# Two transformer blocks on one core: the first rows of each stage by tokens, between the halves of its norm, and three held rows

## The chip, the cores and the metric

The kernel runs on one core of one Trainium2 chip. The metric is device microseconds of one execution, lower being better. The programs are written for the engines TensorE (PE, matrix products), VectorE (DVE), ScalarE (ACT), GpSimd (POOL) and SyncE (SP, which issues most transfers). A scheduler sets the order of each engine's list when the program is built; each engine then works through its list.

## The reference

256 tokens of 1,024 numbers pass through two blocks, each a mixer and a retrieval from 16,384 single-neuron experts ("Peer"). All is float32. Cut to what matters:

```python
# block 1
h = rmsnorm(x, norm_mix_g);  proj = h @ w_in            # 28 tiles of 128 columns
# retention heads (rq, rk, rv, rg) and differential attention heads (dq, dk, dv)
x = x + concatenate([ret_out, diff_out]) @ w_out
x = x + peer(rmsnorm(x, norm_ffn_g), peer_wq, peer_subkeys, peer_u, peer_v)
x = rmsnorm(x, final_norm_g)
# block 2
h = rmsnorm(x, norm1);       proj = h @ w_in_2          # gated delta rule (a_*), hgrn (b_*), gates
mix = sigmoid(g_a) * (o_a @ w_branch_a) + sigmoid(g_b) * (o_b @ w_branch_b)
x = x + mix @ w_out_2
x = x + peer(rmsnorm(x, norm2), w_pq, sub_keys, expert_u, expert_v)
return rmsnorm(x, final_norm)

def peer(x, wq, keys, u, v):
    q = x @ wq                                   # 8 heads x 2 halves x 128
    # top 16 of each half's scores, top 16 of their 256 sums, softmax: gates
    h = gelu(x @ u.T)                            # of the chosen experts
    return (gate * h) @ v
```

## The kernel before

**Stages and rows.** Five stages follow one another: mix1, Peer 1, mix2, Peer 2 and the output. Each streams its weights as rows: a row is one block of 128 x 1024 float32, 512 KB. `plan` lists 684 of them. A row passes through three steps (`_dma`, `_conv`, lines 147 to 168):

- SP fetches it into one of three buffers `raw` (line 151);
- ACT copies it to `hi`, a rounded fp32r value (line 159);
- DVE, and POOL for the last 384 columns in most stages, subtract to get `lo = raw - hi` (line 164).

`hi` and `lo` have three buffers each (the ring). `prefetch(ahead)` converts rows until `ahead` of them lie ahead of use, and issues fetches up to three rows beyond the last conversion. A fetch waits until its buffer's `lo` is done, a conversion until PE has finished with the ring's place.

**Products.** All large products are three fp32r products, hi·hi, hi·lo and lo·hi. `tile_ch` (line 197) makes one tile of 128 output columns for 256 tokens from one row: the weights are stationary, the tokens move, 24 matmuls of 256 columns. `acc_tile` (line 278) is for the output products: the tokens are stationary, the weights move, and a row is added to four PSUM banks `y` by 12 matmuls of 512 columns. At the end of each such stage the last `LAST` = 2 rows are held: `acc_held(0)` adds both to the first 128 tokens, `acc_held(1)` then to the second, so that the first tokens' norm can start while PE works on the second.

**Seams.** A norm (`norm`, `norm_twice`, `norm_first`, `final`) adds `y` to `x` on DVE (lines 289, 291), squares on ACT (296), multiplies by the gain on DVE, makes the reciprocal root on POOL (308) and a diagonal on DVE (300). PE multiplies by it, which transposes and scales at once (323), ACT and DVE evict the result as `xh` and `xl` (325, 326). Both halves of the tokens are normed, then the stage's first row is multiplied. One row of the next stage is converted ahead of the norm, the others behind its last eviction (`prefetch_behind`).

**Background work.** Heads of the mixers, top-k searches and gates are generators. `pass_round` and `step` advance them between rows; they share six PSUM banks. In mix1, `ch`/`cl` are the hi and lo parts of the heads' outputs, the stationary operand of its output projection. In mix2, `mh`/`ml` are those of the gated sum, whose column j comes from branch row b_j, so that branch rows and rows of the output projection alternate.

**Peer.** 16 query rows, 128 rows `u` and 128 rows `v`; in the last part `ah`/`al` are the hi and lo parts of an expert row's activations (lines 634, 635).

## Time and profile before

| what | value |
|---|---|
| median of 3 runs | 2221.36 us (2220.66 to 2223.72) |
| the profiled execution's own time | 2218.6 us |
| its span | 2216.8 us |
| mean granted TensorE clock, as a share of full speed | 0.996 |
| busy: PE, DVE, ACT, POOL | 2167.8, 1533.0, 1154.8, 813.5 us |

A row of a timeline gives the start, the time it took, the engine, the line of the kernel, the operation, the tile written and the tiles read, and in brackets how long the engine had been idle before it and what ended the wait. A row with xN stands for N instructions that follow one another; its time is that of all. The time of one matmul is from its start to its modelled end; matmuls overlap, and how fast they go is read from the distance of their starts.

### The profile page before, as it was taken

The page shows a single profiled execution, that of the slowest core. Times are in us where ns is not written, and L with a number is a line of the kernel's source. Part 1 is how long each engine was busy: PE and PEld are TensorE (multiplying, and loading weights), DVE is VectorE, ACT ScalarE, POOL GpSimd, SP SyncE. Part 2 cuts the span into 40 slices and gives each one's busy share as a digit, 9 for nine tenths or more (in the row PEclk, how much of TensorE's full clock was granted, in tenths as well). Part 3 has the DMA queues.
Part 4 walks back from the last instruction along what each step waited for, and adds up shares of the span by engine and source line. Part 5 has one row for each costly group of instructions (what it writes and reads, how often), then busy time and mean ns, then how long its engine had stood idle before and what let it go on. Part 6 is the DMA issues. An engine that isn't in the chain of part 4 may idle for free. (4 is left out here: it accounts for less than half of the span.)

```text
span 2216.8 us, 41395 instructions
## 1 busy us (share of the span) xinstructions
PE 2167.8 (98%) x15512; PEld 2016.0 (91%) x15512; DVE 1533.0 (69%) x3122; ACT 1154.8 (52%) x2183; POOL 813.5 (37%) x623
## 2 busy tenths in 40 slices
PE   8999999999999999989999999999999999999998
PEld 8989999999988888879899998999999999888887
DVE  5669986898644544477687787799778885444444
ACT  5645545444455555556455655455454445555554
POOL 3454000000065666646275675620000002665664
PEclk9999999999999999999999999999999999999999
DMA  5555655555556656534444244555555555665654
GB/s 188 155 176 162 185 170 167 157 162 161 172 190 207 200 192 196 193 118 137 131 123 135 68 143 152 173 162 185 178 162 158 157 160 183 193 206 190 195 194 152
DMA packets 103880, 370.89 MB, mean 167 GB/s; under 512 B 12928, under 2 KB 14080, under 8 KB 103424
## 3 DMA queue, kind: packets, MB, share of 16 engines
q1 hardware_dynamic: 101808, 365.21, 52.1%
q10 hardware_dynamic: 1872, 3.04, 0.5%
q8 instruction: 122, 2.00, 0.4%
q14 instruction: 78, 0.64, 0.1%
HBM read 367.16 MB, written 1.05 MB: 166 GB/s over the span
## 5 line engine op out<-in xcount | busy, mean ns | idle before, releaser
L164 POOL TENSOR_TENSOR lo<-raw,hi 128x384 fp32r<-128x384 f32 (+1 forms) x428 | 689.5, 1612 | 1309.1 <-ACT hi L159 1271.4
L159 ACT ACTIVATE hi<-raw 128x1024 fp32r<-128x1024 f32 x684 | 724.0, 1060 | 680.2 <-PE mm L197 403.4
L164 DVE TENSOR_TENSOR lo<-raw,hi 128x640 fp32r<-128x640 f32 (+1 forms) x654 | 668.0, 1022 | 313.5 <-ACT hi L159 306.2
L197 PE MATMUL mm<-xh,hi 128*128 128x256 f32 x2848 | 820.9, 288 | 4.4 <-DVE sg L866 2.9
L197 PE MATMUL mm<-xh,lo 128*128 128x256 f32 x2848 | 807.5, 284 | 0.3 <-DVE lo L164 0.2
L197 PE MATMUL mm<-xl,hi 128*128 128x256 f32 x2848 | 803.9, 282 | 0.9 <-DVE xl L326 0.7
L197 PEld LDWEIGHTS mm<-xh,hi 128*128 128x128 f32 x2848 | 538.2, 189 | 5.9 <-DVE sg L866 3.3
L197 PEld LDWEIGHTS mm<-xl,hi 128*128 128x128 f32 x2848 | 538.9, 189 | 1.8 <-DVE xl L326 1.1
L197 PEld LDWEIGHTS mm<-xh,lo 128*128 128x128 f32 x2848 | 534.8, 188 | 0.7 <-DVE lo L164 0.7
L278 PE MATMUL y<-lo,ah 128*128 128x512 f32 x1024 | 398.2, 389 | 0.0
L278 PE MATMUL y<-hi,ah 128*128 128x512 f32 x1024 | 397.4, 389 | 0.0
L278 PE MATMUL y<-hi,al 128*128 128x512 f32 x1024 | 275.9, 389 | 0.0
L635 DVE TENSOR_TENSOR al<-a,ah 128x256 fp32r<-128x256 f32 x256 | 118.1, 462 | 193.2 <-PE y L278 192.9
L278 PEld LDWEIGHTS y<-hi,al 128*128 128x128 f32 x1024 | 192.2, 188 | 39.9
L278 PEld LDWEIGHTS y<-lo,ah 128*128 128x128 f32 x1024 | 192.3, 188 | 39.8
L278 PEld LDWEIGHTS y<-hi,ah 128*128 128x128 f32 x1024 | 192.2, 188 | 39.8
L634 ACT ACTIVATE ah<-a 128x256 fp32r<-128x256 f32 x256 | 106.5, 417 | 168.3 <-PE y L278 166.7
L197 PE MATMUL wm<-xh,hi 128*128 128x256 f32 x320 | 92.1, 289 | 5.4 <-ACT sq L1059 2.1
L197 PE MATMUL wm<-xh,lo 128*128 128x256 f32 x320 | 90.6, 285 | 0.6 <-DVE lo L164 0.6
L197 PE MATMUL wm<-xl,hi 128*128 128x256 f32 x320 | 90.5, 283 | 0.3 <-DVE xl L326 0.3
L535 DVE TENSOR_TENSOR ow<-ow,w 128x1024 f16<-128x1024 f16 x128 | 87.1, 683 | 0.1
L563 ACT ACTIVATE a<-mm 128x256 f32<-128x256 f32 (+33 forms) x228 | 69.0, 302 | 0.0
(513 smaller groups left out, 2271.6 us busy)
## 6 DMA issues: line engine op xcount, KB each, us to landing
raw<-in_u_dram SPq DMA_DIRECT2D x256, 512.0 KB, 3.5
raw<-in_v_dram SPq DMA_DIRECT2D x256, 512.0 KB, 4.2
raw<-in_w_in_dram SPq DMA_DIRECT2D x108, 512.0 KB, 3.5
raw<-in_wq_dram SPq DMA_DIRECT2D x32, 512.0 KB, 3.7
raw<-in_w_out_dram SPq DMA_DIRECT2D x16, 512.0 KB, 3.6
raw<-in_w_branch_a_dram SPq DMA_DIRECT2D x8, 512.0 KB, 3.5
raw<-in_w_branch_b_dram SPq DMA_DIRECT2D x8, 512.0 KB, 3.6
skT<-in_sk_dram ACTq DMA_DIRECT2D x2, 1024.0 KB, 5.1
```

Source lines behind the costliest of these rows:

```text
L159: self.nc.scalar.activation(out=h, in_=r, func=ACTF.Copy)
L164: eng.tensor_tensor(out=l[:, a:b], in0=r[:, a:b], in1=h[:, a:b].bitcast(F32), op=ALU.subtract)
L197: self.nc.tensor.matmul(out=ps, lhsT=a[:, c, :], rhs=b, start=(c == 0 and k == 0), stop=(c == NC - 1 and k == 2))
L278: i = self.nc.tensor.matmul(out=self.y[tt][dh], lhsT=p[:, ts], rhs=q[:, ds], start=(first and m == 0), stop=(last and m == 2))
L535: nc.vector.tensor_tensor(out=ow[q], in0=ow[0], in1=some(self.w[:, q]), op=ALU.mult)
L563: nc.scalar.activation(out=a[:, s, n:T], in_=ps[:, n:T], func=ACTF.Gelu)
L634: nc.scalar.activation(out=h, in_=a, func=ACTF.Copy)
L635: nc.vector.tensor_tensor(out=l, in0=a, in1=h.bitcast(F32), op=ALU.subtract)
```

## The change

The first 512 columns (four rows) of mix1, Peer 1, mix2 and Peer 2 are computed by `tile_tok`: tokens stationary, weights moving, 12 matmuls of 512 columns per row, 6 for each half of the tokens. `seam` puts them between the norms: `prefetch(3)`, norm of the first tokens, three rows for the first tokens, norm of the second tokens, the same rows for the second tokens, then row 4 for both. Since the result has tokens on partitions, mix1's differential values and four of mix2's `b_i` heads need no transposes any more; the first four query tiles of Peer are transposed instead (8 each).

`LAST` is 3. `hold` gives the held rows a home outside the ring, and the run-ahead grows towards a stage's end, so that three rows of the next stage are converted as well. In a norm the gain is multiplied half by half, and the second tokens' work is ordered behind the first's diagonal and last eviction (`turn`). Evictions are in halves, in mix1's first norm in quarters. The rest: `gs` is spread at row 66 of V instead of 40 and multiplied at 88 instead of 60, the `lambda` values of mix1 are made by a generator, and in mix2 `delta` takes its banks in pairs and has fewer steps; the four `b_i` rows that stood after the output gate's are now the stage's first. Line numbers of the change: fetch 152, `hi` 163, `lo` 167, `tile_ch` 206, `tile_tok` 216, adds 328 and 330, squares 339, diagonal 343, evictions 372 and 373.

```diff
     def _conv(self):
         n = self.n_cv
         r = self.raw.pop(n)
-        h = self.ring.tile([P, D], FR, tag="hi", name="hi", bufs=HI)
+        if n in self.place:
+            h, l = self.place.pop(n)
+        else:
+            h, l = (self.ring.tile([P, D], FR, tag=t, name=t, bufs=b) for t, b in (("hi", HI), ("lo", LO)))
         self.nc.scalar.activation(out=h, in_=r, func=ACTF.Copy)
-        l = self.ring.tile([P, D], FR, tag="lo", name="lo", bufs=LO)
...
+    def hold(self, n, homes):
+
+        for m, pair in enumerate(homes):
+            assert self.n_use + n + m >= self.n_cv
+            self.place[self.n_use + n + m] = pair
...
+    def tile_tok(self, tt, w, n, y):
+        h, l = w
+        ts = slice(tt * P, (tt + 1) * P)
+        todo = [(x, b, c2) for x, bs in ((self.xh, (h, l)), (self.xl, (h,))) for c2 in range(2) for b in bs]
+        for m, (x, b, c2) in enumerate(todo):
+            self.last_mm = self.nc.tensor.matmul(out=y, lhsT=x[:, 2 * n + c2, ts], rhs=b[:, c2 * 512:c2 * 512 + 512],
+                                                 start=(n == 0 and m == 0), stop=(n == 3 and m == len(todo) - 1)).ins
+
+    def seam(self, norms, before=3):
+
+        self.prefetch(3)
+        norms[0]()
+        ws = [self.weights() for _ in range(3)]
+        self.quads = [self.bank([P, 512])]
+        for n in range(3):
+            if n == before:
+                norms[1]()
+            self.tile_tok(0, ws[n], n, self.quads[0][1])
+        if before == 3:
+            norms[1]()
+        self.quads.append(self.bank([P, 512]))
+        for n in range(3):
+            self.tile_tok(1, ws[n], n, self.quads[1][1])
+            with self.tc.issue_after(self.last_act):
+                self.prefetch(n + 1)
+        w = self.weights()
+        for tt in range(2):
+            self.tile_tok(tt, w, 3, self.quads[tt][1])
...
         for dh in range(2):
             hs = self.half(dh)
-            self.add_half(tt, dh, None)
-            self.square(x[:, hs], xn[:, hs], s[dh])
-        for dh in range(2):
-            hs = self.half(dh)
-            nc.vector.tensor_tensor(out=xg[:, hs], in0=x[:, hs], in1=gn[:, hs], op=ALU.mult)
+            with self.turn(tt, dh):
+                self.add_half(tt, dh, None)
+                self.square(x[:, hs], xn[:, hs], s[dh])
+                nc.vector.tensor_tensor(out=xg[:, hs], in0=x[:, hs], in1=gn[:, hs], op=ALU.mult)
...
-LAST = 2
+LAST = 3
...
                 for tt in range(2):
                     k.acc_tile(tt, w, a, n == 0, False)
                 k.step(BUD[1])
-                k.prefetch()
+                k.prefetch(2 + max(0, (n - (P - LAST - 9)) // 2))
 
             held = [(k.weights(), a) for a in last]
             i = k.acc_held(0, held)
-            k.prefetch(1)
+            k.prefetch(3)
...
-def out_proj(k, order, ch, cl, ready, last=2):
+def out_proj(k, order, ch, cl, ready, homes):
...
+    k.hold(len(order) - last, homes)
...
-            k.prefetch()
+            k.prefetch(min(3 + n, last + 3))
...
     i = k.acc_held(0, ws)
-    k.prefetch(1)
+    k.prefetch(3)
...
+        for tt, (tag, ps) in enumerate(k.quads):
+            nc.scalar.activation(out=self.bi[:, tt, 0:4, :].rearrange("p h n -> p (h n)"), in_=ps, func=ACTF.Copy)
+            k.done(tag)
...
-        for h in range(H):
+        for h in range(4, H):
             ps = k.tile_ch()
             k.spawn(self.token_value(h, ps))
             after(2)
...
-        for what, j in mix2_out_order():
+        cut = lambda t: [t[:, 4 * n:4 * n + 4, :].rearrange("p a b -> p (a b)") for n in range(2)]
+        k.hold(16 - LAST, [cut(self.oah), cut(self.oal), [self.t([P, D], f"wd{n}", FR, tag=f"dec{n}") for n in range(2)]])
+        for n, (what, j) in enumerate(mix2_out_order()):
+            ahead = 2 + min(LAST + 1, max(0, (n - 4) // 2))
```

What this does to the lists of the engines, at three places.

ACT at the end of mix1 (`hi` and `w_...` are conversions of rows, the latter of held rows in homes outside the ring; `ch` is a head's output, `xn` the norm's squares). Before:

```order
L772 ACTIVATE ch<-fy 128x256
L705 ACTIVATE rv<-by_1445 128x256
L159 ACTIVATE hi<-raw 128x1024
L756 ACTIVATE fj,fss<-bg_1484 128x128 x2
L159 ACTIVATE hi<-raw 128x1024 x4
L772 ACTIVATE ch<-fy 128x256
L159 ACTIVATE hi<-raw 128x1024
L296 ACTIVATE xn,nrm<-x 128x512 x4
```

and in the change:

```order
L844 ACTIVATE ch<-fy 128x256
L772 ACTIVATE rv<-by_1386 128x256
L163 ACTIVATE w_1407<-raw 128x1024
L163 ACTIVATE hi<-raw 128x1024 x2
L828 ACTIVATE fj,fss<-bg_1457 128x128
L163 ACTIVATE w_1409<-raw 128x1024
L828 ACTIVATE fj,fss<-bg_1457 128x128
L163 ACTIVATE w_1411<-raw 128x1024
L163 ACTIVATE hi<-raw 128x1024 x3
L844 ACTIVATE ch<-fy 128x256
L339 ACTIVATE xn,nrm<-x 128x512 x3
```

The last `ch` stood ahead of the one conversion of a Peer row; it now stands behind three of them.

ACT at the end of mix2 (`oah`, `oal` and `wd_...` are the held rows' homes, `mh` a column of the gated sum). Before:

```order
L1522 ACTIVATE mh<-by 128x256
L159 ACTIVATE hi<-raw 128x1024 x2
L1522 ACTIVATE mh<-by 128x256
L159 ACTIVATE hi<-raw 128x1024
L296 ACTIVATE xn,nrm<-x 128x512 x4
```

and in the change:

```order
L1608 ACTIVATE mh<-by 128x256
L163 ACTIVATE oah<-raw 128x1024
L163 ACTIVATE hi<-raw 128x1024
L163 ACTIVATE oal<-raw 128x1024
L1608 ACTIVATE mh<-by 128x256
L163 ACTIVATE wd_15853<-raw 128x1024
L163 ACTIVATE hi<-raw 128x1024 x3
L1608 ACTIVATE mh<-by 128x256
L339 ACTIVATE xn,nrm<-x 128x512 x3
```

The last `mh` likewise stands behind the conversions of three rows of the next stage, and these behind the last held row's.

DVE at the end of Peer 1 (`al` belongs to the last rows of V, `x<-y,x` is the norm's add). Before:

```order
L635 TENSOR_TENSOR al<-a_1722,ah 128x256
L164 TENSOR_TENSOR lo<-raw,hi 128x640 x3
L291 SCALAR_TENSOR_TENSOR x<-y,x 128x512 x2
L385 TENSOR_TENSOR a_4058<-x,a_4058 128x512
```

and in the change:

```order
L167 TENSOR_TENSOR wl_9417<-raw,wh_9416 128x640
L167 TENSOR_TENSOR lo<-raw,hi 128x640
L694 TENSOR_TENSOR al<-a_1742,ah 128x256
L167 TENSOR_TENSOR wl_9419<-raw,wh_9418 128x640
L167 TENSOR_TENSOR wl_9421<-raw,wh_9420 128x640
L167 TENSOR_TENSOR lo<-raw,hi 128x640 x3
L330 SCALAR_TENSOR_TENSOR x<-y,x 128x512 x2
L431 TENSOR_TENSOR x_9410<-x,g_9406 128x512
```

The add stood behind the conversions of two held rows and one row of mix2; it now stands behind three of each.

## Rows read from the trace of the kernel before

**Rows 1.** The page: engines' busy time; groups of instructions with mean ns and idle time.
```profile
PE 2167.8 (98%) x15512; PEld 2016.0 (91%) x15512; DVE 1533.0 (69%) x3122; ACT 1154.8 (52%) x2183; POOL 813.5 (37%) x623
...
L164 POOL TENSOR_TENSOR lo<-raw,hi 128x384 fp32r<-128x384 f32 (+1 forms) x428 | 689.5, 1612 | 1309.1 <-ACT hi L159 1271.4
L159 ACT ACTIVATE hi<-raw 128x1024 fp32r<-128x1024 f32 x684 | 724.0, 1060 | 680.2 <-PE mm L197 403.4
...
L278 PE MATMUL y<-lo,ah 128*128 128x512 f32 x1024 | 398.2, 389 | 0.0
```

**Rows 2.** Stretches: length, busy PE, PEld, DVE, ACT, POOL, then clock, DMA share, GB/s.
```profile
140.00:143.00 3.00, 0.77 (x4) 0.29 (x2) 3.00 (x8) 1.93 (x6) 0.56 (x1) 1.00 0.52 183
...
952.00:958.00 6.00, 0.41 (x3) 0.14 (x1) 5.45 (x15) 3.54 (x10) 1.08 (x3) 0.72 0.12 48
958.00:960.00 2.00, 2.00 (x10) 2.00 (x11) 0.29 (x1) 0.02 (x1) 2.00 (x3) 0.50 0.00 0
960.00:962.00 2.00, 2.00 (x13) 2.00 (x13) 0.69 (x1) 0.89 (x2) 1.23 (x2) 0.62 0.00 0
962.00:964.00 2.00, 1.66 (x15) 1.46 (x14) 1.49 (x4) 1.41 (x4) 0.36 (x1) 1.00 0.00 0
1398.00:1400.00 2.00, 0.84 (x4) 0.36 (x2) 2.00 (x5) 1.01 (x3) 0.56 (x1) 1.00 0.51 201
```

**Rows 3.** Timeline of PE, mix1 to Peer 1.
```profile
140.15 0.40 PE L278 MATMUL y<-lo,ch 128*128 128x512 f32 x1
140.38 0.39 PE L278 MATMUL y<-hi,cl 128*128 128x512 f32 x1
143.22 2.02 PE L323 MATMUL bg<-xn,xg 128*128 128x128 f32 x16 [2.45 <-DVE xn L300]
...
147.55 0.39 PE L197 MATMUL mm<-xl,hi 128*128 128x256 f32 x1 [0.34 <-DVE xl L326]
147.78 0.28 PE L197 MATMUL mm<-xh,lo 128*128 128x256 f32 x1
147.90 0.28 PE L197 MATMUL mm<-xh,hi 128*128 128x256 f32 x1
```

**Rows 4.** Timeline of PE, Peer 1 to mix2.
```profile
951.91 0.39 PE L278 MATMUL y<-hi,al 128*128 128x512 f32 x1
957.89 3.76 PE L323 MATMUL bg<-a 128*128 128x128 f32 x16 [5.59 <-issue]
...
963.95 0.39 PE L197 MATMUL wm<-xl,hi 128*128 128x256 f32 x1 [0.34 <-DVE xl L326]
```

**Rows 5.** Timeline of PE, mix2 to Peer 2.
```profile
1398.45 0.39 PE L278 MATMUL y<-hi,ml 128*128 128x512 f32 x1
1400.61 2.02 PE L323 MATMUL bg<-xn,xg 128*128 128x128 f32 x16 [1.77 <-DVE xn L300]
...
1404.94 0.39 PE L197 MATMUL mm<-xl,hi 128*128 128x256 f32 x1 [0.34 <-DVE xl L326]
```

**Rows 6.** Timeline of ACT, the output projection of mix1.
```profile
124.58 1.06 ACT L159 ACTIVATE hi<-raw 128x1024 fp32r<-128x1024 f32 x1 [3.40 <-PE y L278]
...
126.19 2.00 ACT L159 ACTIVATE hi<-raw 128x1024 fp32r<-128x1024 f32 x2
131.14 1.06 ACT L159 ACTIVATE hi<-raw 128x1024 fp32r<-128x1024 f32 x1 [2.96 <-DMA raw<-in_w_out_dram]
133.91 1.06 ACT L159 ACTIVATE hi<-raw 128x1024 fp32r<-128x1024 f32 x1 [1.71 <-DMA raw<-in_w_out_dram]
134.88 0.40 ACT L772 ACTIVATE ch<-fy 128x256 fp32r<-128x256 f32 x1
```

**Rows 7.** DMA issues from 126 to 146 us: KB each, median us from issue to landing.
```profile
raw<-in_wq_dram SPq DMA_DIRECT2D x4, 512.0 KB, 4.3
raw<-in_w_out_dram SPq DMA_DIRECT2D x2, 512.0 KB, 3.9
```

**Rows 8.** Timeline of ACT, the output projection of mix2.
```profile
1376.59 1.06 ACT L159 ACTIVATE hi<-raw 128x1024 fp32r<-128x1024 f32 x1 [1.37 <-PE y L278]
...
1390.45 1.06 ACT L159 ACTIVATE hi<-raw 128x1024 fp32r<-128x1024 f32 x1 [1.63 <-PE mm L197]
1391.44 0.42 ACT L1522 ACTIVATE mh<-by 128x256 fp32r<-128x256 f32 x1
1393.35 1.06 ACT L159 ACTIVATE hi<-raw 128x1024 fp32r<-128x1024 f32 x1 [1.49 <-PE y L278]
```

**Rows 9.** Timeline of ACT, last rows of Peer 1.
```profile
936.07 1.06 ACT L159 ACTIVATE hi<-raw 128x1024 fp32r<-128x1024 f32 x1 [0.54 <-PE y L278]
...
938.79 1.06 ACT L159 ACTIVATE hi<-raw 128x1024 fp32r<-128x1024 f32 x1 [0.54 <-PE y L278]
```

**Rows 10.** Timeline of DVE, the start of Peer 1's norm.
```profile
948.04 0.83 DVE L164 TENSOR_TENSOR lo<-raw,hi 128x640 fp32r<-128x640 f32 x1 [1.90 <-ACT hi L159]
949.17 1.29 DVE L291 SCALAR_TENSOR_TENSOR x<-y,x 128x512 f32<-128x512 f32 x2 [0.30 <-PE y L278]
```

**Rows 11.** Timeline of ACT, the output's norm.
```profile
2210.41 0.72 ACT L304 ACTIVATE a<-a,nrm 128x512 f32<-128x512 f32 x1
2211.03 0.61 ACT L296 ACTIVATE a<-x 128x512 f32<-128x512 f32 x1
```

**Rows 12.** The stretch of mix2 with its last `mx` tiles, columns as in rows 2.
```profile
1340.00:1360.00 20.00, 16.83 (x120) 14.35 (x120) 15.54 (x32) 9.79 (x30) 11.49 (x12) 1.00 0.41 147
```

More of the change, by code (lines that the diff above doesn't have):

```diff
@@ L319, in transposed @@
             tag, ps = self.bank([P, 4, P])
-            cs = slice(c4 * 4, c4 * 4 + 4)
+            with self.tc.issue_after(self.last_mm) if tt else nullcontext():
+                for c in range(4):
+                    cc = c4 * 4 + c
+                    nc.tensor.matmul(out=ps[:, c, :], lhsT=x[:, cc * P:(cc + 1) * P], rhs=dr, start=True, stop=True)
+            for c in range(0, 4, 2):
+                cs = slice(c4 * 4 + c, c4 * 4 + c + 2)
+                h, v = self.xh[:, cs, ts], ps[:, c:c + 2]
+                last = nc.scalar.activation(out=h, in_=v, func=ACTF.Copy)
+                i = nc.vector.tensor_tensor(out=self.xl[:, cs, ts], in0=v, in1=h.bitcast(F32), op=ALU.subtract).ins
@@ new lines, in transposed, with norm_first @@
+            self.done(tag)
+        self.last_act = last.ins
+        self.behind[1] = i
+    def norm_first(self, tt, g, xn):
+        nc = self.nc
+        x, s = self.x[:, tt, :], self.columns()
+        self.square(x[:, 512:D], xn[:, 512:D], s[0])
+        nc.vector.scalar_tensor_tensor(out=xn[:, 0:512], in0=x[:, 0:512], scalar=1.0 / D, in1=x[:, 0:512],
+                                       op0=ALU.mult, op1=ALU.mult, accum_out=s[1])
+        nc.vector.tensor_scalar(out=s[4], in0=s[0], scalar1=s[1], scalar2=EPS, op0=ALU.add, op1=ALU.add)
+        self.rsqrt(s[6], s[4])
+        dr = xn[:, 0:P]
+        self.diagonal(dr, s[6])
+        ts = slice(tt * P, (tt + 1) * P)
+        for c4 in range(2):
+            tag, ps = self.bank([P, 4, P])
+            with self.tc.issue_after(self.last_mm) if tt else nullcontext():
+                for c in range(4):
+                    cc = c4 * 4 + c
+                    nc.tensor.matmul(out=ps[:, c, :], lhsT=x[:, cc * P:(cc + 1) * P], rhs=dr, start=True, stop=True)
@@ L412, in final @@
             hs = self.half(dh)
-            self.add_half(tt, dh, scale)
-            self.square(x[:, hs], xn[:, hs], s[dh])
-        for dh in range(2):
-            hs = self.half(dh)
-            nc.vector.tensor_tensor(out=xg[:, hs], in0=x[:, hs], in1=gb[:, hs], op=ALU.mult)
+            with self.turn(tt, dh):
+                self.add_half(tt, dh, scale)
+                self.square(x[:, hs], xn[:, hs], s[dh])
+                nc.vector.tensor_tensor(out=xg[:, hs], in0=x[:, hs], in1=gb[:, hs], op=ALU.mult)
         nc.vector.tensor_scalar(out=s[4], in0=s[0], scalar1=s[1], scalar2=EPS, op0=ALU.add, op1=ALU.add)
@@ L736, in mix1 @@
     with k.tc.tile_pool(name="m1", bufs=1) as pool:
-        k.norm_first(k.g, [pool.tile([P, D], F32, name="xn", tag="xn", bufs=2) for tt in range(2)])
-        k.prefetch_behind()
+        k.seam([lambda tt=tt: k.norm_first(tt, k.g, pool.tile([P, D], F32, name="xn", tag="xn", bufs=2)) for tt in range(2)], 2)
+        vt = pool.tile([P, 2, 4, P], F32, name="vt")
+        for tt, (tag, ps) in enumerate(k.quads):
+            nc.scalar.activation(out=vt[:, tt].rearrange("p h n -> p (h n)"), in_=ps, func=ACTF.Copy)
+            k.done(tag)
+        k.prefetch()
         half = k.const(pool, "half", True)
@@ L1537, in run @@
         xg, xn = self.t([P, 2, D], "xg", tag="bi"), self.t([P, 2, D], "xn", tag="sgb")
-        for tt in range(2):
-            k.norm(tt, gn, xg[:, tt], xn[:, tt])
-        k.prefetch_behind()
+        k.seam([lambda tt=tt: k.norm(tt, gn, xg[:, tt], xn[:, tt]) for tt in range(2)])
     def both(self):
@@ L1611, in program @@
         mix2(k)
-        Peer(k, 2, "final_norm_2").run(lambda *a: k.final(*a[:5], out))
+        Peer(k, 2, "final_norm_2").run(lambda *a: k.final(*a, out))
 def _tiles(w):
```

202 lines of the change are left out of this document (106 added, 96 removed).

## The prediction

> **What bounds the kernel now.** The profile's page comes first: TensorE (PE) is busy for 98% of the span [rows 1]. Taking work off another engine therefore gains nothing by itself. Only two things can count: PE's own work, and the places where PE stands still. The seams between stages are read next, in a table of stretches [rows 2]. PE is busy for 0.77 of 3 us behind mix1, 0.41 of 6 us behind Peer 1 and 0.84 of 2 us behind mix2. PE's timeline gives the edges [rows 3 to 5]:
>
> - **B**, mix1 to Peer 1: the last `y` product starts at 140.38, the transposes of the new norm at 143.22, the stage's steady products at 147.55.
> - **C**, Peer 1 to mix2: 951.91, 957.89, 963.95.
> - **D**, mix2 to Peer 2: 1398.45, 1400.61, 1404.94.
>
> Products of 512 columns stand 0.23 us apart and those of 256 columns 0.12 [rows 3]. Four rows of 24 narrow ones take 11.5 us, so a seam's first four rows end about 11.4 us behind its steady start: 18.4 us behind the end E of the last `y` product in B, 17.7 in D, 23.2 in C.
>
> Last come the rows that convert weights, on ScalarE (ACT) and GpSimd (POOL) [rows 6 to 8]. They matter because the change wants three rows of the next stage converted ahead of norm 0, beside three held rows: some four conversions more than now, early. One conversion costs ACT 1.06 us and POOL 1.6 [rows 1, 6], against 2.7 us that PE takes for a row. The engines have room. What has little is `raw`, with its three buffers: row n+3 is fetched only when `lo` of row n is done. In rows 6 ACT converts row 3 of the output projection at 124.58, rows 4 and 5 from 126.19 on, row 6 at 131.14 and row 7 at 133.91, both waiting for their DMA. **A buffer's turn** is thus 131.14 - 124.58 = 6.6 us, and 133.91 - 126.19 = 7.7 us where POOL had a queue: 1.06 for `hi`, 1.65 for `lo`, 3.9 to 4.3 from issue to landing [rows 7]. Three rows per 6.6 us is 2.2 us a row; ahead of PE that wins half a microsecond a row, no more. SP issues in order too: no row of the next stage passes a held one.
>
> **The change, part by part, against the profiled execution of 2218.6 us.**
>
> *Token tiles.* 48 products of 512 columns (48 x 0.2266 = 10.9 us, from 12 in 2.72 us [rows 9]) stand for 96 of 256 (11.5): 0.6 us less per seam. Ideal seam: norm 0 lies under the held rows, then 16 transposes 2.0 us [rows 3], eviction 0.8, 18 products 4.1, 2.0 and 0.8 and 4.1 for the second tokens, 2.7 for row 4 = 16.5 us behind E. That is 1.9 less than now in B and 1.1 less in D.
>
> *B.* In ACT's new order `ch` of the last retention head stands behind the conversions of query rows 0 to 2; now it stands ahead of row 0, at 134.88 [rows 6]. ACT works through its list in order, so `ch` starts when query row 2 has landed. The chain of its buffer is rows 4, 7, then query row 2, at 126.2, 133.9 and, one turn later, 140.5 to 141.6. Take 141.0: `hi` ends at 142.1, `ch` (0.40 us) at 142.5. PE needs `ch` for the last held row of the first tokens, behind which 6 + 18 products are left: 140.6 - 24 x 0.2266 = 135.2. It waits from there to 142.5: **+7.3 us**. All that is queued behind that product waits with it: the second tokens' held rows, the norm's add, every transpose. A clock that falls is added: after 5.6 us of standing still in C PE was granted 0.50 for 2 us and its first 16 transposes took 3.76 us instead of 2.02, while after 2.5 and 1.8 us nothing fell [rows 2 to 5]. For 7.3 us I add the 1.7. B = 7.3 + 1.7 - 1.8 (1.9 less a 0.1 wait for norm 0) = **+7.2**; between -1.9 (nothing blocks) and +8.5 (7.7 per turn).
>
> *D.* The same in mix2's output. `mh` of column 7 now runs at 1391.44, ahead of query row 0 at 1393.35 [rows 8]; in the new order it stands behind query rows 0 to 2. The chain: branch row 6 is converted at 1376.59 and held row 5, in its buffer, one turn later, at 1383.1; branch row 7 follows at 1384.2; its `lo` follows that of held row 5 on POOL (to 1387.4), so held row 7 lands at 1390.9, and query row 2 one turn later, at 1397.5; `hi` to 1398.6, `mh` to 1399. PE needs it at 1398.7 - 24 x 0.2266 = 1393.2: +5.6. For the clock 1.0, between the 0 seen after 2.5 us and the 1.7 after 5.6. D = 5.6 + 1.0 - 1.1 = **+5.5**; between -1.1 and +7.
>
> *C.* Nothing of Peer's own stands behind the next stage's rows; the norm does. The add of the first tokens, now at 949.17 behind one `lo` [rows 10], stands behind three. The last one's raw lands about 951.3 (row 124, converted at 936.07 now [rows 9], comes behind held row 125, at about 938.1, then two turns of 6.6), its `lo` ends at 953.3. Six operations on 512 columns at 0.6 us, the statistics, POOL's power and the diagonal put the transposes at 958.7, where they now start at 957.89. PE's clock falls as now. What the hidden second norm saves is given back here: **+0.5**, between -5 (rows land early, transposes 1.5 us behind E) and +2.
>
> *Start.* The transposes of the first tokens start at the same time; walking through conversions and evictions gives four rows done some 0.5 us sooner: **-0.5**, between -2 and +1 (16 evictions of 128 columns instead of 8 of 256).
>
> *End.* No seam follows. The third held row's conversion stands in a chain of raw turns again; I take a wait of 1.5 and 0.5 back, as a square on ACT is now held up by the scaling of the first tokens [rows 11]: **+1.0**, 0 to +3.
>
> *Transposes.* Each Peer gains 8 of query tiles, mix1 loses 8 of values, mix2 loses 8: **0**, within 0.6 either way.
>
> *mix2.* Its last four `b_i` rows keep their place, the first four move to the head. The chain of `hgrn` heads that runs under this stage's products loses four rows of cover, 11.5 us, and more of it comes to lie behind the last `mx` tile, where PE now is busy for 16.83 of 20 us [rows 12]. Against that the new order mixes two branch tiles into the end, and `delta` gives up a row's worth of steps. Walking the heads through by the durations of today gives about as much waiting as now: **+1**, -1 to +7.
>
> *Added early in V:* `gs` is spread at row 66, multiplied on POOL at 88; PE waits for nothing there [rows 1], so **0**; without that cover it would be one POOL product.
>
> Sum: 7.2 + 5.5 + 0.5 - 0.5 + 1.0 + 0 + 1 = **+14.7**: 2233.3 us for an execution like the profiled one. That one lies 2.8 under the median of the runs shown (2221.36), so the forecast is **2236**.
>
> The Trainium skill ("DMA: Bandwidth & Descriptors", its fit of fixed cost and bytes) puts a DMA at about 2.0 us plus bytes over 436 GB/s, an estimate of 3.2 us for 512 KB. The rows show 3.9 to 4.3 in B [rows 7], and they decide; by the page's figure two links of each chain in B and D would be 0.7 to 1.1 shorter, and the sum some 3.5 us lower.
>
> **The rivals.**
>
> *The run-ahead keeps up: faster.* Place: the buffers of `raw` at B, C and D. For it: the held rows no longer wait for a place in the ring, and the engines that convert are idle half of the time. Then B gives -1.9, C -5, D -1.1, start -0.5, end 0, mix2 and the rest +1: -7.5, some **2214**. It decides at one point: the conversion of query row 2 must start 1.5 us (`hi` and `ch`) before the last held row is wanted, in B by 133.7, which needs two turns from 126.2 of 3.7 us each. Rows 6 show 6.6 and 7.7. Against it, too: rows 3 to 5 of the projection start on ring places that PE frees, and these don't come sooner.
>
> *Only one blocks, or the turns are short.* If one seam keeps its turn and the other finds `ch` or `mh` in time, or C comes out at its good end: 14.7 - 7.2 - 5.5 = 2 to 14.7 - 5.5 = 9.2, so 2223 to 2231, and down to 2219 if both turns are short: around **2225**.
>
> *The cover of mix2 is missed as well.* If the heads' chain is bound by latency, four rows of 2.9 us less cover show up by half, +6: **2243**. For it: that stage has waits in its last part already [rows 12].
>
> **How the numbers follow.** Both blocks as worked out: 0.54, 2228 to 2242. Run-ahead keeps up: 0.20, 2208 to 2217. One block: 0.16. Cover missed as well: 0.10, around 2243. About 0.2% (4.4 us) is what a measurement of this kernel can tell from no change. Faster by more than that, under 2216.9: 0.18 of the 0.20. Same: the rest of it and 0.11 of the third case, 0.13. Slower: 0.69. The range leaves out half of the fast case and some of the slowest: 2212 to 2244. The likeliest case's own range is 2228 to 2242.
>
> **What would show it.** In the changed profile, ACT should have the last `ch` at about 142 and the last `mh` some 6 us behind where it stands now, each right behind a `hi` that waited for a DMA; PE should stand 5 to 7 us inside the held rows of both output projections, with a low granted clock behind at least the first; the first tokens' transposes should follow the last held row at once in B and D, and by 5 to 6 us in C. A `hi` of query row 2 that ends before 135 in B, or transposes in C by 955, would prove the core of this wrong.

## The result and the profile after

The change is slower by 0.8%: 2240.1 us (median of 6 executions, 2236.88 to 2240.66) where the kernel before had 2221.81 on the same chip (6 executions, 2220.66 to 2223.72), a ratio of 1.0078 with a 95% interval of 1.0065 to 1.0091. Forecast were 2236 and a range of 2212 to 2244, with 0.69 for slower. The execution that the profiler took lasted 2238.63 us, with a span of 2236.9 us (before 2216.8) and a mean granted clock of 0.988 (before 0.996).

The page of the profile after first, with the busy times and the fetches of query rows with their median from issue to landing:

```profile
PE 2176.6 (97%) x15320; PEld 2014.6 (90%) x15320; DVE 1533.2 (69%) x3148; ACT 1160.5 (52%) x2191; POOL 813.4 (36%) x623
...
raw<-in_wq_dram SPq DMA_DIRECT2D x32, 512.0 KB, 4.1
```

PE has 192 instructions fewer than in [rows 1] and is busy 8.8 us longer: part of its work ran slower. The other engines were busy about as long as before (ACT 5.7 us longer). So the time went into stops of PE and into what follows them. The places are read next, in the order of the prediction.

**B.** ACT's timeline in the output projection of mix1 (start, time, engine, line, operation, and in brackets the idle time before it and what ended it). `w` is the last held row in its home, the three `hi` are query rows 0 to 2 of Peer 1:

```profile
129.15 1.06 ACT L163 ACTIVATE w<-raw 128x1024 fp32r<-128x1024 f32 x1 [0.88 <-DMA raw<-in_w_out_dram]
131.54 1.06 ACT L163 ACTIVATE hi<-raw 128x1024 fp32r<-128x1024 f32 x1 [1.33 <-DMA raw<-in_wq_dram]
134.15 1.06 ACT L163 ACTIVATE hi<-raw 128x1024 fp32r<-128x1024 f32 x1 [1.55 <-DMA raw<-in_wq_dram]
136.90 1.06 ACT L163 ACTIVATE hi<-raw 128x1024 fp32r<-128x1024 f32 x1 [1.69 <-DMA raw<-in_wq_dram]
137.87 0.40 ACT L844 ACTIVATE ch<-fy 128x256 fp32r<-128x256 f32 x1
```

The last `ch` stands behind query row 2, as the order said, and each `hi` ahead of it waited for its DMA. From the last held row at 129.15 to query row 2 at 136.90, which has the same buffer, a turn took 7.75 us. PE's timeline at the same place:

```profile
132.78 0.48 PE L317 MATMUL y<-w,cl 128*128 128x512 f32 x1
138.32 2.07 PE L317 MATMUL y<-w,ch 128*128 128x512 f32 x4 [5.05 <-ACT ch L844]
...
146.39 0.39 PE L317 MATMUL y<-w,cl 128*128 128x512 f32 x1
146.62 1.95 PE L368 MATMUL bg<-xn,xg 128*128 128x128 f32 x16
```

PE stood until `ch` came: 138.32 - 132.78 less one product's 0.23 = 5.3 us. The 24 products left, 24 x 0.23 = 5.6 us at full speed, then took from 138.32 to 146.62, which is 8.3. The transposes, which in [rows 3] come 2.84 us behind the last `y`, follow it at once: norm 0 lies under the held products, as it was meant to.

**C, and the clock at all three seams.** Stretches (length, busy PE, PEld, DVE, ACT, POOL, then granted clock, DMA share, GB/s):

```profile
132.00:138.00 6.00, 1.26 (x7) 0.76 (x5) 2.27 (x5) 2.76 (x4) 3.27 (x2) 0.94 0.76 236
138.00:140.00 2.00, 1.68 (x4) 1.16 (x4) 1.96 (x2) 0.26 (x1) 1.64 (x1) 0.50 0.69 233
140.00:142.00 2.00, 2.00 (x6) 1.60 (x6) 1.15 (x2) 0.42 (x1) 0.00 (x0) 0.50 0.58 162
142.00:144.00 2.00, 2.00 (x6) 1.55 (x5) 1.47 (x4) 0.92 (x4) 0.45 (x1) 0.50 0.33 135
144.00:146.00 2.00, 2.00 (x10) 1.60 (x9) 1.52 (x3) 0.55 (x2) 0.10 (x1) 0.98 0.00 0
956.00:962.00 6.00, 0.37 (x2) 0.00 (x0) 4.88 (x10) 2.97 (x9) 2.17 (x2) 0.82 0.66 210
962.00:964.00 2.00, 1.52 (x7) 1.55 (x8) 1.91 (x4) 0.72 (x2) 0.02 (x1) 0.50 0.03 8
...
1406.00:1412.00 6.00, 0.45 (x2) 0.01 (x1) 3.05 (x5) 3.13 (x4) 3.85 (x3) 0.87 0.70 211
1412.00:1414.00 2.00, 1.79 (x4) 1.49 (x5) 1.58 (x2) 0.16 (x1) 0.56 (x1) 0.50 0.67 219
```

Behind each of the three stops the clock is granted at 0.50, the lower of its two levels (1.2 of 2.4 GHz). In C, DVE adds the first tokens' `y` only behind the third converted row, and PE transposes 6.5 us behind the last `y` (before 5.98, [rows 4]):

```profile
956.30 0.83 DVE L167 TENSOR_TENSOR lo<-raw,hi 128x640 fp32r<-128x640 f32 x1 [1.92 <-ACT hi L163]
957.04 1.28 DVE L330 SCALAR_TENSOR_TENSOR x<-y,x 128x512 f32<-128x512 f32 x2
```

```profile
955.98 0.39 PE L317 MATMUL y<-wh,al 128*128 128x512 f32 x1
962.48 1.83 PE L368 MATMUL bg<-x,x 128*128 128x128 f32 x7 [6.11 <-DVE x L343]
```

**D.** In mix2's output the last `mh`, which in [rows 8] runs right behind its branch tile, stands behind query row 2. ACT, then PE:

```profile
1410.24 1.06 ACT L163 ACTIVATE hi<-raw 128x1024 fp32r<-128x1024 f32 x1 [0.54 <-DMA raw<-in_wq_dram]
1411.74 0.42 ACT L1608 ACTIVATE mh<-by 128x256 fp32r<-128x256 f32 x1 [0.44 <-DVE by L1607]
```

```profile
1412.21 2.07 PE L317 MATMUL y<-wd,mh 128*128 128x512 f32 x4 [5.75 <-ACT mh L1608]
...
1419.95 0.40 PE L317 MATMUL y<-wd,ml 128*128 128x512 f32 x1
1420.19 1.95 PE L368 MATMUL bg<-xn,xg 128*128 128x128 f32 x16
```

The `mh` did not wait for ACT alone. Its input `by` comes from DVE, and DVE's list has the same conversions in it:

```profile
1409.74 0.83 DVE L167 TENSOR_TENSOR lo<-raw,hi 128x640 fp32r<-128x640 f32 x1 [2.13 <-ACT hi L163]
1410.48 0.42 DVE L1606 TENSOR_TENSOR by<-mm,gb 128x256 f32<-128x256 f32 x1
```

The last product of the branch tile ran at 1404.54, but DVE multiplied the tile only at 1410.48, behind the `lo` of query row 1, which had waited for that row's `hi`. In this trace the tile `by` came last, 0.44 us after ACT had finished the `hi` of query row 2; in e9's it is ACT's list that comes last. In B it was ACT's list too: DVE's `fy`, behind the `lo` of query row 1 too, was done at 136.40, and `ch` ran at 137.87.

**Where the 20 us of span went.** Points on PE's timeline were taken in both traces: the last matmul of mix1's last tile, the end of each seam's fourth row, the first and the last `y`. In the kernel before other products stand among the four rows (eight of the search in B and in D; in C 26 small ones of mix2's gates, and a wait); there the fourth row is put at the rows' steady start plus the 11.4 us that four rows take by themselves.

| piece | before | after | difference | forecast |
|---|---|---|---|---|
| start to mix1's last tile | 116.35 | 114.24 | -2.1 | -0.5 |
| B: from there to the fourth row of Peer 1 | 42.6 | 47.8 | +5.2 | +7.2 |
| the two Peers up to their last `y` | | | +2.0 | 0 |
| C: last `y` of Peer 1 to the fourth row of mix2 | 23.4 | 24.7 | +1.3 | +0.5 |
| mix2, from there to its output's first `y` | 387.3 | 395.1 | +7.8 | +1 |
| D: first `y` of that output to the fourth row of Peer 2 | 53.7 | 59.9 | +6.2 | +5.5 |
| end, behind the last `y` | 7.5 | 7.2 | -0.3 | +1 |
| sum | | | +20.1 | +14.7 |

Two stretches went as forecast in kind. mix2 didn't: it lost eight microseconds where one was expected. The experiments had to tell why, and whether the place of the conversions in the engines' lists is what stops PE in B and D.

### The profile page after: what moved, and what is told of

Read it like the earlier page. It is cut to its first block, busy times and chain, and to the rows that moved or that the text cites. A ratio compares the mean times of both kernels' runs of the same rounds, so it can differ in the third digit from the quotient of the medians.

```text
span 2236.9 us, 41026 instructions
## 1 busy us (share of the span) xinstructions
PE 2176.6 (97%) x15320; PEld 2014.6 (90%) x15320; DVE 1533.2 (69%) x3148; ACT 1160.5 (52%) x2191; POOL 813.4 (36%) x623
## 5 line engine op out<-in xcount | busy, mean ns | idle before, releaser
L167 POOL TENSOR_TENSOR lo<-raw,hi 128x384 fp32r<-128x384 f32 (+1 forms) x416 | 672.7, 1619 | 1298.2 <-ACT hi L163 1275.4
L163 ACT ACTIVATE hi<-raw 128x1024 fp32r<-128x1024 f32 x672 | 711.9, 1060 | 685.7 <-PE mm L206 391.5
L206 PE MATMUL mm<-xh,hi 128*128 128x256 f32 x2768 | 798.9, 289 | 10.6 <-DVE cva L1113 3.5
L206 PE MATMUL mm<-xh,lo 128*128 128x256 f32 x2768 | 786.2, 284 | 0.2 <-DVE lo L167 0.2
L206 PE MATMUL mm<-xl,hi 128*128 128x256 f32 x2768 | 781.9, 282 | 0.0
L206 PEld LDWEIGHTS mm<-xh,hi 128*128 128x128 f32 x2768 | 524.0, 189 | 12.3 <-issue 3.7
L206 PEld LDWEIGHTS mm<-xl,hi 128*128 128x128 f32 x2768 | 525.3, 190 | 0.3
L206 PEld LDWEIGHTS mm<-xh,lo 128*128 128x128 f32 x2768 | 521.1, 188 | 0.7 <-DVE lo L167 0.4
L206 PE MATMUL wm<-xh,hi 128*128 128x256 f32 x272 | 77.8, 287 | 3.9 <-ACT hi L163 1.9
L206 PE MATMUL wm<-xl,hi 128*128 128x256 f32 x272 | 76.6, 282 | 0.0
L606 ACT ACTIVATE a<-mm 128x256 f32<-128x256 f32 (+16 forms) x232 | 70.7, 305 | 0.0
```

Source lines behind the costliest of these rows:

```text
L163: self.nc.scalar.activation(out=h, in_=r, func=ACTF.Copy)
L167: eng.tensor_tensor(out=l[:, a:b], in0=r[:, a:b], in1=h[:, a:b].bitcast(F32), op=ALU.subtract)
L206: self.nc.tensor.matmul(out=ps, lhsT=a[:, c, :], rhs=b, start=(c == 0 and k == 0), stop=(c == NC - 1 and k == 2))
L606: nc.scalar.activation(out=a[:, s, n:T], in_=ps[:, n:T], func=ACTF.Gelu)
```

## The experiments

All kernels were timed against the kernel before on one chip per batch. The batches are e1 to e4 (kernel before 2219.59 us), e5 to e8 (2220.43), e9 to e11 (2220.67) and e12 (2219.64). Over these 82 executions the kernel before lay between 2215.54 and 2225.30, so single executions tell little below 5 us, and medians and intervals carry the verdicts.

**e1: the next stage's rows behind the last `ch` and `mh`.** The change, but the conversions of query rows are ordered behind the output projection's own last operations, in B and in D. The order holds for ACT's `hi` and for DVE's `lo` alike, so the two lists are not told apart:

```diff
-                nc.scalar.activation(out=ch[:, c, :], in_=y, func=ACTF.Copy)
+                i = nc.scalar.activation(out=ch[:, c, :], in_=y, func=ACTF.Copy)
...
+                k.tail = i.ins, j.ins
...
-            k.prefetch(min(3 + n, last + 3))
+            k.prefetch(min(3 + n, len(order) - n - 1))
...
-    k.prefetch(3)
+    with k.tc.issue_after(k.tail[0]), k.tc.issue_after(k.tail[1]):
+        k.prefetch(3)
```

> The change with one thing undone: at the end of mix1 and of mix2 the next stage's three rows are converted behind the last ch/cl and mh/ml instead of ahead of them (the run-ahead stops at the stage's own rows). Theory Q (the wait is the place in ACT's list): PE's waits for the last ch (5.3 us) and the last mh (some 6 us) inside the held rows vanish, the granted clock stays at 1.0 there, and 8 us of the 18 come back, since the first norm's squares still stand behind query row 2: about 2232. Theory W (PE waits for weights: the held rows themselves come too late through three raw buffers): the waits stay, about 2240.

Measured: 2233.78 us (4 executions), ratio 1.0073 (1.0056 to 1.0090), span 2230.9. ACT and PE in B:

```profile
135.25 0.42 ACT L845 ACTIVATE ch<-fy 128x256 fp32r<-128x256 f32 x1 [2.81 <-DVE fy L844]
135.57 1.99 ACT L163 ACTIVATE hi<-raw 128x1024 fp32r<-128x1024 f32 x2
138.53 1.06 ACT L163 ACTIVATE hi<-raw 128x1024 fp32r<-128x1024 f32 x1 [0.97 <-DMA raw<-in_wq_dram]
139.50 0.61 ACT L339 ACTIVATE xn<-x 128x512 f32<-128x512 f32 x1
```

```profile
135.71 1.20 PE L317 MATMUL y<-w,ch 128*128 128x512 f32 x4 [0.73 <-ACT ch L845]
143.99 2.02 PE L368 MATMUL bg<-xn,xg 128*128 128x128 f32 x16 [2.42 <-DVE xn L343]
```

The stop of 5.05 us is down to 0.73 and no clock falls in B. B takes 43.6 us instead of 47.8, D 54.6 instead of 59.9: the 9.5 us come from the place of `ch` and `mh`, and of their inputs, in the lists. What is next is seen in the same rows. Norm 0's square (139.50) now stands behind the three conversions, and the transposes come 2.8 us behind the last `y` (141.18). The total alone would not have shown this: the ratios of e1 and of the change overlap, and in e1's trace mix1's last tile was 1.7 us later and mix2 2.7 us longer. The seams were repaired, and the rest of the slowdown was not in them.

**e2: the kernel before with four `b_i` rows at the head of mix2,** which takes four rows of cover from the end of the stage and nothing else:

```diff
         next(k.spawn(self.columns()))
+        for h in range(4):
+            ps = k.tile_ch()
+            k.spawn(self.token_value(h, ps))
+            after(2)
...
-        for h in range(H):
+        for h in range(4, H):
```

> The kernel before with one part of the change alone: mix2's first four b_i rows stand at the head of the stage, as ordinary tiles of 256 columns with their transposes; delta, norms and held rows are untouched. Theory C (cover): the hgrn heads lose four rows of products to run under, mix2 gets 5 to 9 us longer, about 2229. Theory Y (what made mix2 7.9 us longer is delta's taking banks in pairs): no difference beyond 2 us from before, about 2222.

Measured: 2220.16 us (10 executions), ratio 1.0004 (0.9995 to 1.0014). The theory of the lost cover falls as the cause of mix2's eight microseconds: the stretch from Peer 1's last `y` to the output's first took 412.9 us, where the kernel before has 410.7 and the change 419.8.

**e3: e1, and norm 0's squares ahead of two of the three rows** in B and D. e1's ordered `prefetch(3)` becomes a `prefetch(1)`, and in `seam`:

```diff
-        self.prefetch(3)
-        norms[0]()
+        if before == 2:
+            self.prefetch(3)
+            norms[0]()
+        else:
+            self.prefetch(1)
+            norms[0]()
+            with self.tc.issue_after(self.sq), self.tc.issue_after(self.behind[0]):
+                self.prefetch(3)
```

> e1, and at those two seams only the first row of the next stage is converted ahead of the first norm, the other two behind its squares and its diagonal. Theory Q: the norm's squares no longer stand behind query row 2, so the first transposes come some 4 us sooner at each of the two seams than in e1: 2226 to 2230. Theory W: as e1, about 2240.

Measured: 2228.62 us (4 executions), ratio 1.0047 (1.0031 to 1.0064). In B, PE's first transpose now stands 0.67 us behind the last `y` (139.02):

```profile
139.69 2.02 PE L374 MATMUL bg<-xn,xg 128*128 128x128 f32 x16 [0.28 <-DVE xn L349]
```

B takes 42.5 us and D 53.8, where the kernel before takes 42.6 and 53.7. So with both places in the lists put right, the seams are as long as they were, not shorter. And 0.47% were still missing.

**e4: the change without mix2's token tiles,** `b_i` at its old place, no early row of mix2 in Peer 1; `delta` is as in the change:

```diff
-            if k.n_use < len(k.plan):
-                k.seam(norms)
+            for f in norms:
+                f()
...
-        for h in range(4, H):
+        for h in range(H):
```

> The change without mix2's token tiles: at the seam of Peer 1 to mix2 both norms, then rows as before; b_i in its old place; delta keeps its pairs; V of Peer 1 converts no row of mix2 early. The waits for ch and mh stay. Theory C: the 7.9 us of mix2 and the 1.3 us of its seam go, 2230 to 2233. Theory Y: delta's pairs are still there, mix2 stays long, 2238 or more.

Measured: 2239.59 us (4 executions), ratio 1.0089 (1.0072 to 1.0106). The stretch through mix2 stays at 419.9 us. Neither the token tiles nor `b_i`'s place makes it long; of the change's edits inside that stretch `delta`'s new steps were left to try.

**e5 and e9: `delta`'s old steps,** put into e3 (e5) and into the change itself (e9). The change's steps differ in two ways, two banks asked for at once and half as many steps; "the pairs" below means both together, and they were not tried apart. Three places of this form:

```diff
-        yield from k.need(2)
-        banks = [k.bank([P, 4, P]) for tt in range(2)]
-        for tt, (bt, px) in enumerate(banks):
+        for tt in range(2):
+            yield from k.need(1)
+            bt, px = k.bank([P, 4, P])
             for h in range(4):
                 nc.tensor.transpose(out=px[:, h, :], in_=X[:, tt, h, :], identity=k.ident)
-        yield
-        for tt, (bt, px) in enumerate(banks):
+            yield
             nc.scalar.activation(out=XT[:, tt], in_=px, func=ACTF.Copy)
```

> e3 with delta's steps as before (one bank at a time); mix2 keeps its token tiles. Since the loss of cover alone cost nothing, theory Y (delta's pairs) stands against theory Z (cover and the token head together: the hgrn heads' chain reaches the end of the stage late, whatever delta does). Y: mix2 gets 5 to 8 us shorter than in e3, 2221 to 2224. Z: within 2 us of e3, about 2228.

> The change with delta's old steps (banks one at a time, a step each) and nothing else altered. Theory P: the pairs cost what they cost between e3 and e5, some 4 to 5 us, in the stretch from the last y of Peer 1 to the first y of mix2's output, whatever the seams do: 2240 - 4.5 = 2235.5 (ratio 1.0055 to 1.0075 where the change has 1.0078), and that stretch falls from 419.8 to some 414 us in the trace. Rival I: the pairs cost only what e6's median showed on the kernel before, 1.7 us or less, and the gain of e5 came out of the reordering of queues around it: 2238 to 2240, stretch 418 or more.

Measured: e5 2224.56 us (10 executions), ratio 1.0017 (1.0007 to 1.0027); e9 2231.64 (6 executions), ratio 1.0047 (1.0033 to 1.0061). They lie 0.30 and 0.31% below the kernels that they were made from (1.0047 and 1.0078), some 6.7 us; theory P had expected less, 4 to 5 us and a ratio of 1.0055 to 1.0075 for e9. mix2's stretch falls to 414.1 and 413.6 us, as Y and P had it.

**e6 and e12: the kernel before with the pairs alone,** the same edit the other way round; e12 is the same kernel, timed again.

> The kernel before with delta's new steps alone. Y: mix2 5 to 8 us longer than before, about 2226. Z: as before, within 2 us.

> The kernel of e6 once more (the kernel before with delta's new steps alone), since its median showed 1.7 us (interval -1.3 to +3.8) while its one trace showed a mix2 ten microseconds longer. Theory P: the pairs cost time in themselves, by stops of PE of 1.4 to 3.5 us in mix2 that are followed by a granted clock of 0.50; then 2223 to 2226, ratio 1.001 to 1.0025 with its interval above 1. Rival I: they cost only beside the change's other parts; then within 1 us, interval on both sides of 1.

Measured: e6 2222.1 us (10 executions), ratio 1.0006 (0.9994 to 1.0017); e12 2223.28 (11 executions), ratio 1.0013 (1.0004 to 1.0023). By e6's median the pairs alone cost nothing that can be told, though its one trace, which is the slowest of its ten executions, has a stretch of 420.9 us. By the second measurement they cost something, 0.9 to 5.1 us, and by both medians less than inside the change. Of the rows in which PE waits (what waits, for what; us in total, times, longest), e12 has this one, which the kernel before hasn't:

```profile
PE mm L197 <- DVE cva L1037: 3.5, 1, 3.5
```

**e7: e5 without mix2's token tiles,** the edit of e4 again. It leaves the seams B and D, three held rows and the homes.

> e5 without mix2's token tiles and b_i in its old place, and with no row of mix2 converted ahead of Peer 1's last norm: what is left of the change are the token tiles of mix1 and both Peers, the held rows and the order of the norms. Y and Z alike: mix2 is as long as before, so only the seams count: start -2, B -3, D 0 to -1, two Peers +1.8, C 0: 2215 to 2219, that is 2 to 4 us faster than before. If mix2 is still 5 us longer, both theories fall and the cause is in its output stage or its seam.

Measured: 2221.81 us (10 executions), ratio 1.0008 (0.9998 to 1.0018): what is left of the change is worth nothing that can be told, and the 2 to 4 us that were expected of the seams did not come.

**e8, e10 and e11: one row instead of three ahead of the norm in C too.** e8 is e5 with this edit, e11 the same kernel again, and e10 is e8 with the pairs put back.

```diff
-                k.prefetch(2 + max(0, (n - (P - LAST - 9)) // 2))
+                k.prefetch(min(2 + max(0, (n - (P - LAST - 9)) // 2), P - n - 1))
...
-            k.prefetch(3)
+            k.prefetch(1)
```

> e5, and at the seam of Peer 1 to mix2 too only one row of the next stage is converted ahead of the first norm's squares. Theory Q (the norm's add and squares stand behind row 2 of the next stage): the first transposes come 2 to 4 us sooner than in e5 there, and so does the end. If PE waits for the rows' weights instead, no gain or a loss of up to 2.

> e8 with the pairs put back: all seams as in e8, delta as in the change. Theory P: 4 to 5 us above e8 in this batch, ratio to the kernel before 1.0018 to 1.0025, stretch from last y of Peer 1 to first y of mix2's output 413 or more where e8 had 408.8. Rival I: within 2 us of e8, ratio under 1.001, stretch under 411.

> The kernel of e8 once more, as the yardstick for e10 on the same chip, and for the question whether what is left of the change is worth anything. If the seams' gain shows (its trace ended 2.5 us before that of the kernel before): 2218, ratio 0.999. If it is given back by extra transposes and limited run-ahead: ratio 1.000 as in the first measurement.

Measured: e8 2220.2 us (10 executions), ratio 0.9999 (0.9989 to 1.0010); e11 2218.77 (11 executions), 0.9986 (0.9977 to 0.9995); e10 2224.17 (12 executions), 1.0015 (1.0006 to 1.0025). C falls from 24.4 us in e5 to 20.9 in e8 and 21.1 in e11: the transposes come 2.7 us behind the last `y` in e8 (950.23 to 952.94), not 6.5. The pairs cost 5.4 us between e11 and e10, in one batch and with nothing else changed. e8 and e11 are the best versions of the change; they are level with the kernel before to within 0.15% (e11's interval lies below 1, e8's on both sides of it).

**What the pairs do** was read in e10 against e11. PE's waits from 970 to 1376 us, the two that cost most in e10, and then the one in e11:

```profile
PE mm L206 <- ACT ob L1492: 3.6, 2, 3.0
PE mm L206 <- DVE cva L1121: 3.5, 1, 3.5
```

```profile
PE mm L206 <- ACT mx L1593: 3.7, 2, 3.2
```

The stop of 3.5 us, as DVE and PE saw it in e10:

```profile
1066.99 0.47 DVE L1121 SCALAR_TENSOR_TENSOR cva<-mm,i_conv_a,cva 128x255 f32<-128x255 f32 x1
1067.38 0.92 DVE L1358 TENSOR_TENSOR svm<-svL,svY 128x128 f32<-128x128 f32 x1
1068.22 0.47 DVE L1121 SCALAR_TENSOR_TENSOR cva<-mm,i_conv_a,cva 128x254 f32<-128x254 f32 x1
1068.62 0.27 DVE L1359 TENSOR_REDUCE svY<-svm 128x16 f32<-128x128 f32 x1
1068.81 0.47 DVE L1121 SCALAR_TENSOR_TENSOR cva<-mm,i_conv_a,cva 128x253 f32<-128x253 f32 x1
```

```profile
1065.64 0.28 PE L206 MATMUL mm<-xh,lo 128*128 128x256 f32 x1
1069.42 0.55 PE L206 MATMUL mm<-xh,hi 128*128 128x256 f32 x1 [3.50 <-DVE cva L1121]
1069.77 0.41 PE L206 MATMUL mm<-xl,hi 128*128 128x256 f32 x1
1069.98 0.41 PE L206 MATMUL mm<-xh,lo 128*128 128x256 f32 x1
```

A projection tile wants a PSUM bank `mm` that the convolution `cva` still reads, and DVE's three reads stand between steps of `delta`'s solve (`svm`, `svY`). The stop goes with the pairs: all seven traces of kernels that have them show it, 3.5 or 3.6 us long, between 1060 and 1080 us, with a granted clock of 0.50 behind it. In the seven without them no `mm` waits for `cva`, and the longest stop between 1040 and 1100 us is 2.4 us. How the pairs bring the solve's steps between these reads was not followed. Behind the stop the products stand 0.21 us apart instead of 0.12. The stretches of e10, and the first of them in e11, show the clock:

```profile
1066.00:1068.00 2.00, 0.00 (x0) 0.00 (x0) 2.00 (x5) 1.36 (x4) 0.84 (x1) 1.00 0.41 139
1068.00:1070.00 2.00, 0.58 (x3) 0.61 (x4) 2.00 (x6) 0.42 (x1) 0.15 (x1) 0.65 0.66 256
1070.00:1072.00 2.00, 2.00 (x11) 2.00 (x11) 1.90 (x7) 0.00 (x0) 0.00 (x0) 0.50 0.27 55
```

```profile
1066.00:1068.00 2.00, 2.00 (x19) 2.00 (x18) 2.00 (x6) 0.59 (x3) 1.01 (x1) 1.00 0.70 213
```

For all kernels this was summed over mix2, from Peer 1's last `y` to the first `y` of the output. "Idle" is the time in which PE did nothing; "lost to the clock" is, for each microsecond from 20 us into the stretch on, PE's busy time times what the granted clock lacked of 1.

| kernels | stretch, us | idle, us | lost to the clock, us |
|---|---|---|---|
| without pairs: before, e2, e5, e7, e8, e9, e11 | 408.8 to 414.1, mean 411.8 | 25.2 to 30.2, mean 27.3 | 1.7 to 4.8, mean 3.3 |
| with pairs: the change, e1, e3, e4, e6, e10, e12 | 419.1 to 422.5, mean 420.3 | 27.4 to 31.3, mean 29.0 | 6.2 to 14.6, mean 9.6 |

The two groups don't overlap in the first and the last column. Of the 8.5 us between them, 6.3 are clock and 1.7 are idle time. One trace per kernel stands behind each row, and those of e6 and e10 are the slowest executions of their kernels, so the 8.5 us are more than the 5.4 to 6.9 that the medians give for the pairs inside the change. The mean granted clock of all executions of e10 (0.991 to 0.994, 12 of them) and e11 (0.995 to 0.997, 11 of them) says the same without the traces. With the pairs alone it spreads from 0.992 to 0.998 (e6 and e12): some executions lose next to nothing to the clock.

## Why the prediction was right, and where it was not

**The core held.** `ch` and `mh` (or, for `mh`, its input on DVE) stood behind conversions that wait for DMAs, PE stood inside the held rows for 5.3 and 5.9 us, the clock fell behind both stops, the transposes followed at once in B and D and 6.5 us behind in C. e1 takes these places in the lists away, and with them the stops and 9.5 us of seam. The marks named for "wrong" (a query row 2 by 135, transposes in C by 955) stayed away.

**B, +7.2 forecast, +5.2 measured.** Three terms of its sum were off.

- The wait: 7.3 forecast, 5.3 measured. The turn of a buffer was right, 7.75 us against 6.6 to 7.7. What failed was the step before it, "the chain of its buffer is rows 4, 7, then query row 2", at today's 133.9 for row 7. `ch` came at 137.87, not 142.1. Of these 4.2 us 2.1 are this execution's earlier start of the stage, and PE wants `ch` sooner by as much (133.0, not 135.2). The other 2 are what the homes do: the first held row, row 5, needs no place in the ring and is converted ahead of rows 3 and 4, which wait for PE. Its `raw` buffer comes free first, so the last held row follows row 3 and not row 4 (SP issues the three fetches behind row 5 at 123.54, 125.51 and 127.07, each as the `lo` of rows 5, 3 and 4 ends):

```profile
120.72 1.06 ACT L163 ACTIVATE w<-raw 128x1024 fp32r<-128x1024 f32 x1 [1.44 <-DMA raw<-in_w_out_dram]
122.69 2.01 ACT L163 ACTIVATE hi<-raw 128x1024 fp32r<-128x1024 f32 x2 [0.90 <-PE y L317]
```

- The clock: 1.7 forecast, 2.7 measured. The 1.7 was what 16 transposes lost in C [rows 4]; 24 products of 512 columns lay behind this stop.
- The seam's own gain: 1.8 forecast, 2.8 by what is left (5.3 + 2.7 - 5.2). That counts also the waits which the stop hides; the repaired seam of e3 has 1.3 behind the last `y`.

The Trainium skill ("DMA: Bandwidth & Descriptors", the section on the anatomy of one DMA) gives its fit of fixed cost and bytes for transfers that GpSimd issues; taken for SP's, it would make a fetch of 512 KB an estimate of 3.2 us. The trace does not agree, with a median of 4.1 over the 32 query rows. The shorter wait in B is no sign for the page's figure, since the turn was at the long end.

**D, +5.5 forecast, +6.2 measured.** The walk through the chain gave `mh` at 1399; with the 13.2 us by which the stage's output began later, that is 1412.2, and it ended at 1412.16. So close a hit is partly luck: the last held row was converted 1.0 us sooner than in the walk, the turn behind it took 7.2 us and not 6.6, and what ended last was DVE's `by`, which the walk had left out. The wait was 5.9 us (the last product before it starts at 1406.06, so 1412.21 - 1406.06 less 0.23), forecast 5.6 (5.8 by the walk's own points, 1399 and 1393.2). The clock took 2.4 instead of 1.0: the 24 products from 1412.21 to 1420.19 are 8.0 us where 5.6 are right at full speed. What is left as the seam's own gain is 2.1 us, forecast 1.1, again with the waits that the stop hides.

**C, +0.5 forecast, +1.3 measured.** `lo`, adds and transposes came within half a microsecond of their forecast distances behind the last `y`. e8 confirms that it is the two extra conversions which hold the norm back: without them C is 3.4 us shorter.

**mix2, +1 forecast, +7.8 measured: the step that failed.** The text had "walking the heads through by the durations of today gives about as much waiting as now". By the means of the two groups that nearly holds, 29.0 against 27.3 us of idle time; in the change itself it is 30.3 against the 26.3 of the kernel before. But it counted waits as a sum, and the time depends on how they lie and on what the clock does behind them: in these traces the stops of 2.6 to 3.6 us in mix2 have a stretch at 0.50 behind them. `delta` was entered only as "gives up a row's worth of steps" at no price of its own, and in every trace the long stage goes with its pairs. The rival "the cover of mix2 is missed as well" had this size, +6, and a cause that e2 refutes; with token tiles at the head too, e5's stretch is 414.1 us against 412.5 without them in e7.

**Start, -0.5 forecast.** In 14 traces mix1's last tile lies between 112.9 and 116.9 us, with and without the change, so the -2.1 in the table is the spread of executions and no effect of the change. **End, +1.0 forecast, -0.3 measured:** no wait for the third held row showed. **Peers, 0 forecast, +2.0 measured:** the prediction's 0 was a balance over the whole kernel, in which mix1 and mix2 lose what the Peers gain. The two Peers are 0.9 and 1.1 us longer here, about what eight query transposes cost by the 2.0 us of the 16 in [rows 3]; what the mixers gained lies in other rows of the table.

So the total came out within 4.1 us of the median partly by luck: mix2 was 6.8 us too low, and B, the start and the end together 4.9 us too high. The measured time lies nearer to the 2243 of the rival on mix2's cover than to 2236, for another reason than that rival's, and a range of 2212 to 2244 would have held a faster kernel as well.

**The account of the 0.78%,** by ratios to the kernel before. `delta`'s pairs are 0.30% (0.31% from the change to e9, 0.30% from e3 to e5, 0.29% from e11 to e10). The place of the last `ch`, `mh` and of norm 0's squares in the lists is another 0.30% (e9 to e5; by the lengths of the seams e1 carries most of it, 9.5 us in its trace, while its ratio alone does not tell it from the change). The two extra rows ahead of the norm in C are 0.18% (e5 to e8) to 0.31% (to e11). Nothing is left over that can be told from the noise, each ratio being known to 0.1 or 0.2%: token tiles, three held rows and homes come to 0.9999 and 0.9986. That the ideal seams' gain of 1.9 and 1.1 us did not come out of B and D even when both were repaired (42.5 and 53.8 us against 42.6 and 53.7) can be placed: in e3 the part behind the last `y` is 1.3 and 0.6 us shorter than before, and the output projection ahead of it 1.2 and 0.6 us longer, 0.73 and 0.34 of that a wait for `ch` and `mh` left inside the held rows. Why the pairs cost twice as much inside the change as alone stays open, and so does whether a fourth `raw` buffer would have kept the conversions ahead, which wasn't tried.

## What to carry to other kernels

When work for the next stage is pulled forward on an engine that works through a list, ask which operation of the present stage, and which input of it on another engine, now stands behind it and what that work waits for: here a transfer of four microseconds ahead of a 0.4 us copy cost five on the engine that was full. Price a stop of TensorE by its own length and then by what is left to do at the lower clock behind it, and do not sum waits over a stage: in these traces a stage with 1.7 us more idle time was eight microseconds longer, six of them by the clock. And when a change of many parts is slower, take the parts out one by one until nothing is left, since the part that looked like housekeeping (banks in pairs) cost as much as the one that was feared.
